# A streaming encoder layer on one core: last super-block's key and value rows through VectorE and DRAM, its last two projections unsplit, its last row tile scaled on two engines

## The chip, the cores and the metric

The kernel runs on one core of a Trainium2 chip. The core has a matrix engine (TensorE, "PE" in the profile, with its weight loads as "PEld"), VectorE (DVE), ScalarE (ACT), GpSimd (POOL), a queue engine SyncE (SP) that issues almost all transfers here, and 16 DMA engines. The metric is the device time of one execution in microseconds; less is better. Every engine works through its own queue of instructions in order and waits on semaphores of the others.

## The reference

One layer of a hybrid encoder over 2048 prompt frames and 64 frames of a running stream. A combined projection feeds two groups of heads; their gated outputs are concatenated and projected back. The keys and values of the last 512 prompt frames are outputs too (`new_k_prompt`, `new_v_prompt`), in row order.

```python
aq, ak, av, ag, hq, hf, hi, hg = split(rms_norm(x, ln_g) @ w_in)   # x: 2048 (64) x 1024, w_in: 1024 x 4096
o_a = band_attention(aq, ak, av) * silu(ag)      # 8 heads x 64, chunks of 64 frames see 8 chunks back
o_b = rms_norm(gla_recurrence(silu(hq), 1 - f, hi, log f)) * silu(hg)   # 4 heads x 128, f from sigmoid(hf)
y   = rms_norm(x + concat(o_a, o_b) @ w_out)     # also returned: the last 512 rows of k and v, the states
```

## The kernel before

**Stages.** The frames are cut into four super-blocks of 512 frames (the second has the 64 sample frames as well, `SUPER`). In each, 32 projection jobs run, listed in `JOBS`: for each of four recurrence heads the jobs hf, hq, hi, hg, and for each of four pairs of attention heads pg (gate), pq, pk, pv. A job is 24 accumulating matmuls with 128 features as the stationary operand and up to 512 frames as the moving one (`project`, L539): activations and weights are each split in a high and a low part, and three of the four products are summed. The result lands transposed, features on partitions and frames along the row, in one of two accumulator banks ("acc"), and an `ev_...` function takes it out. Matmuls of attention and recurrence are woven between the projection's. In the last super-block the jobs of the last pairs come in another order: hf3, hq3, pv2, pq2, pk2, hi3, hg3, pg2, pv3, pq3, pk3, pg3. Then the output projection runs for all eight tiles of 256 rows (`steps`, with seven products of a Strassen-like scheme for each), its sums are added to the residual rows on VectorE and GpSimd, and `out_norm` squares, normalizes and stores each tile of 128 rows.

**What sets the order.** All instructions are emitted by one Python program (`Plan`) that keeps a model clock with costs for each engine, and threads (generators) that ask for tokens. `tk["sig"]` and the like count the buffers of a tag; a thread takes a token before it uses a buffer, and `put(1, t)` gives it back at model time `t`. So the planner's due times fix the order of each engine's queue; on the chip, semaphores wait for the real event. Tags that matter here: "sig" (two buffers of 128x512, used by the exponentials of the gates and of hf, hq and hg, and as staging for output rows), "vT" (three such buffers, used by q, k, v and the recurrence's inputs), "ck" (one buffer, used for the squares of the norms among others), "tr" (two PSUM banks for transposes), "kv0" and "kv1" (the one set of key and value tiles, given on from pair to pair).

**Keys and values in the first three super-blocks.** `ev_k` (L790) copies the accumulator to a vT tile and splits it for both heads into the key tile. `ev_v` needs frames on partitions, so it transposes 32x32 blocks on VectorE (`turn_blocks`, L666), sends them through a DRAM scratch called "way" with four writes and one read back (`turn_rows`, L677, L691 and L695), and splits the rows (`split_rows`, L657). The recurrence's inputs (hi) take the same way.

**In the last super-block**, `ev_v_last` (L811) copies the values to a vT tile and turns them on TensorE, four half-height transposes for each head, and `new_rows` (L624) turns the whole tile once more, four transposes of 128x128, copies the result to a sig tile (L645) and stores it with one transfer (L650). `ev_k` calls the same `new_rows` for the keys. The sig token comes back as soon as the store is issued.

**The last two jobs** of every super-block (and its first two) run in two halves of 256 frames: job n-2 first half, job n-1 first half, then both second halves, so that the next super-block's activations can replace the first half early.

**The end.** For the last pair of row tiles, `out_norm` scales each tile's two 512-wide halves one after the other on VectorE, by the row's factor and by the gain, and SP stores each half (L1898, L1901).

Of the kernel before, what the change touches and what calls it, by code (L numbers as in the profile page):

```python
# [183 lines left out]
def hymba_step(  # L184
# [439 lines left out]
    def new_rows(src, off, bn, p, out_p, out_s, tok, t):  # L624
# [15 lines left out]
        for a, b, rows, out in segs:  # L640
            s3 = pt[:rows, a * P : b * P].rearrange("p (t d) -> p t d", d=P)
            yield from tk["sig"].get()
            yield "D", t
            st = T(wk, [P, 512], F32, "sig", bufs=2).rearrange("p (t d) -> p t d", d=P)
            dve.tensor_copy(st[:rows, : b - a], s3)  # L645
            t = C.dve((b - a) * P)
            yield t
            row = off + a * P
            if rows == P:
                sp.dma_start(out[row : row + (b - a) * P, p * P : (p + 1) * P].rearrange("(t q) d -> q t d", q=P),  # L650
                             st[:, : b - a])
            else:
                sp.dma_start(out[:, p * P : (p + 1) * P], st[:rows, 0])
            tk["sig"].put()
        tk["tr"].put(1, t)

# [82 lines left out]
    def pair_jobs(sb, p):  # L739
        t0, n = SUPER[sb][:2]  # L740
        last = sb == len(SUPER) - 1
        smp = n > WIN
# [47 lines left out]
        def ev_k(acc, off, bn, t):  # L790
# [17 lines left out]
            yield from new_rows(kn, off, bn, p, nk_prompt if last else None, nk_sample, tk["vT"], t)  # L808
# [31 lines left out]
        def ev_v(acc, off, bn, t):  # L840
# [9 lines left out]
            for c, w, rows, out in parts:  # L850
                if out is not None:
                    rows_out(vt[:rows, c : c + w], out, slice(p * P, (p + 1) * P), t)
            for h in range(2):
                yield lambda: d.open[h]
                for c, w, rows, _ in parts:
                    yield "A", t
                    t = yield from split_rows(vt[:rows, c : c + w], d.v, h, 4 + (off + c) // P, w // P, rows, t)
                d.v_n[h] += bn
                d.v_t[h] = max(d.v_t[h], t + 500.0)
            tk["vT"].put(1, t)  # L860
# [43 lines left out]
        return d, dict(g=ev_g, q=ev_q, k=ev_k, v=ev_v_last if last else ev_v)  # L904
# [956 lines left out]
    def out_norm(o, tile_, half, t):  # L1861
# [11 lines left out]
        if tile_ not in o["first"]:  # L1873
# [5 lines left out]
            o["b0"][tile_] = b0  # L1879
            return  # L1880
# [6 lines left out]
        if x[3] is not None and not end:  # L1887
# [5 lines left out]
            C.dma(512 * rows / P)  # L1893
        else:
# [56 lines left out]
    def program():  # L1951
# [66 lines left out]
        for sb in range(nsb):  # L2018
# [6 lines left out]
            for u, (kind, g) in enumerate(JOBS[sb]):  # L2025
# [16 lines left out]
                if u in (1, len(JOBS[sb]) - 1):  # L2042
# [7 lines left out]
                elif u not in (0, len(JOBS[sb]) - 2):  # L2050
                    yield from project(j, blocks, evac)
                before = evac
# [149 lines left out]
```

## Time and profile before

| what | value |
|---|---|
| median of 3 runs | 1247.86 us (1247.58 to 1248.82) |
| the profiled execution's own time | 1248.42 us |
| its span, first to last instruction | 1246.1 us |
| mean granted TensorE clock | 0.999 |
| TensorE busy | 99% of the span, 7494 matmuls |
| VectorE, ScalarE, GpSimd busy | 72%, 55%, 33% |
| DMA, queue of SP | 289.86 MB, 69.0% of 16 engines' time |

The profile lists for each group of instructions the line of the kernel that issued it, the engine, the operation, the output and input tiles, and the shape; then the busy time, the mean duration of one, and the idle time ahead of it with what ended that. The time line has start, duration, engine, line and count of merged instructions. Matmuls overlap in the pipeline, so what one costs in a stream is the distance between starts and not its duration.

### The profile page before, as it was taken

To read this page: it belongs to the slowest core of one execution; us is meant where nothing else is said; L and a number is where in the kernel's file an instruction comes from. 1 tells how busy PE (TensorE), PEld (TensorE's weight loads), DVE (VectorE), ACT (ScalarE), POOL (GpSimd) and SP (SyncE) were. 2 spreads that over 40 slices of the span, in tenths; PEclk is the share of its full clock that TensorE was granted. 3 is DMA by queue.
4 is the path that set the end of the run, shared out by engine and by line. 5 is a ranking of instruction groups with operands and counts; after the bars stand their busy time and mean duration, and the time that the engine had idled before them with its cause. 6 is when DMAs were issued, how large, how long until landed. Compare 5 with 4: busy or idle time off the path is not lost. (4 is left out here: it accounts for less than half of the span.)

```text
span 1246.1 us, 21403 instructions
## 1 busy us (share of the span) xinstructions
PE 1234.7 (99%) x7494; PEld 1085.9 (87%) x7494; DVE 893.0 (72%) x1901; ACT 683.0 (55%) x1534; POOL 413.2 (33%) x702
## 2 busy tenths in 40 slices
PE   9999999999999999999999999999999999999997
PEld 7888888999999999998888888988888888888786
DVE  7697878867767677786577667776757476867775
ACT  6354545755665556574465556665556445643443
POOL 7665564111120111201233242143242103474543
PEclk9999999999999999999999999999999999999999
DMA  8897888667575575655777778677686665988431
GB/s 337 301 321 258 320 293 327 204 185 252 155 217 148 158 252 186 204 164 189 279 267 251 271 263 281 227 257 252 231 273 206 218 209 208 343 266 245 144 118 68
DMA packets 144516, 291.22 MB, mean 234 GB/s; under 512 B 38617, under 2 KB 85337, under 8 KB 126746
## 3 DMA queue, kind: packets, MB, share of 16 engines
q1 hardware_dynamic: 144120, 289.86, 69.0%
q8 instruction: 59, 0.97, 0.3%
q14 instruction: 47, 0.39, 0.1%
q10 hardware_dynamic: 290, 0.01, 0.0%
HBM read 196.95 MB, written 93.91 MB: 233 GB/s over the span
## 5 line engine op out<-in xcount | busy, mean ns | idle before, releaser
L249 PE MATMUL acc<-xh,w 128*128 128x512 f32 (+2 forms) x2752 | 566.0, 345 | 1.2 <-DVE gq L580 0.7
L249 PEld LDWEIGHTS acc<-xh,w 128*128 128x128 f32 x2752 | 438.4, 189 | 51.7 <-ACT xh L409 0.9
L249 PE MATMUL acc<-xl,w 128*128 128x512 f32 (+2 forms) x1376 | 293.8, 345 | 0.5 <-DVE xl L415 0.5
L249 PEld LDWEIGHTS acc<-xl,w 128*128 128x128 f32 x1376 | 221.0, 189 | 25.2 <-DVE xl L415 0.7
L939 ACT ACTIVATE pr<-pr,nm 128x640 f32<-128x640 f32 (+4 forms) x132 | 100.4, 761 | 56.3 <-DVE nm L922 55.9
L951 ACT CAST ph<-tr 128x512 fp32r<-128x512 f32 (+3 forms) x176 | 87.8, 506 | 74.8 <-PE pv L249 50.1
L922 DVE CUSTOM_DVE_ANT_0 pr<-s,bias 128x640 f32<-128x640 f32 (+4 forms) x128 | 94.3, 737 | 46.6 <-PE s L249 45.7
L473 POOL TENSOR_TENSOR w<-wraw,w 128x256 fp32r<-128x256 f32 x120 | 102.3, 882 | 54.9 <-DVE w L468 41.8
L954 DVE TENSOR_TENSOR ph<-tr,ph 128x512 fp32r<-128x512 f32 (+3 forms) x176 | 100.8, 588 | 25.0 <-ACT ph L951 24.3
L249 PE MATMUL pv<-ph,v 128*128 128x256 f32 (+2 forms) x344 | 97.1, 368 | 0.0
L510 POOL TENSOR_TENSOR xn<-wraw,xn 128x256 fp32r<-128x256 f32 x48 | 41.2, 859 | 145.0 <-ACT xn L507 145.0
L253 PE MATMUL tr<-ident,pr 128*128 128x128 f32 x580 | 88.3, 273 | 0.3 <-DVE ph L954 0.3
L1570 POOL TENSOR_TENSOR k<-ob 128x512 f32<-128x512 f32 (+2 forms) x20 | 18.0, 902 | 198.4 <-ACT ob L1561 157.3
L1095 POOL TENSOR_TENSOR mixa<-mixa,sga 128x256 f32<-128x256 f32 (+1 forms) x36 | 28.0, 779 | 167.1 <-DVE mixa L993 141.4
L993 DVE TENSOR_TENSOR mixa<-mixa,pv 64x256 f32<-64x256 f32 (+1 forms) x144 | 56.8, 394 | 35.7 <-ACT mixa L989 32.2
L943 DVE TENSOR_SCALAR pr<-pr,sm 128x640 f32<-128x640 f32 (+4 forms) x132 | 75.8, 574 | 4.7
L253 PEld LDWEIGHTS tr<-ident,pr 128*128 128x128 f32 x580 | 69.6, 140 | 9.9 <-PE acc L249 0.7
L575 ACT ACTIVATE sig<-acc 128x512 f32<-128x512 f32 (+2 forms) x64 | 32.0, 500 | 76.4 <-PE acc L249 73.7
L249 PEld LDWEIGHTS pv<-ph,v 128*128 128x128 f32 (+1 forms) x344 | 58.6, 189 | 7.4 <-issue 0.3
L989 ACT COPY mixa<-pv 64x256 f32<-64x256 f32 (+1 forms) x72 | 25.1, 349 | 64.3 <-PE pv L249 58.4
L249 PE MATMUL s<-kd,q 128*128 128x320 f32 (+2 forms) x232 | 55.6, 309 | 0.0
L249 PE MATMUL s<-kd,ql 128*128 128x320 f32 (+2 forms) x232 | 55.5, 309 | 0.0
(338 smaller groups left out, 2131.2 us busy)
## 6 DMA issues: line engine op xcount, KB each, us to landing
w<-wd SPq DMA_DIRECT2D x96, 1024.0 KB, 5.4
wd<-w SPq DMA_DIRECT2D x32, 1024.0 KB, 7.1
wraw<-in_w_in_dram SPq DMA_DIRECT2D x30, 512.0 KB, 5.0
wod<-xn SPq DMA_DIRECT2D x28, 512.0 KB, 5.0
xn<-in_x_prompt_dram SPq DMA_DIRECT2D x23, 512.0 KB, 4.7
bias<-biasd SPq DMA_DIRECT2D x24, 320.0 KB, 5.8
carry<-kd SPq DMA_DIRECT2D x12, 512.0 KB, 5.8
carry<-v SPq DMA_DIRECT2D x12, 512.0 KB, 6.2
```

The costliest lines, as they stand in the source:

```text
L249: pe.matmul(out, w, x, **kw)
L253: pe.transpose(out, x, idn)
L473: pool.tensor_sub(w[:, 1, k : k + 2], raw[:, k : k + 2], f32(w[:, 0, k : k + 2]))
L510: pool.tensor_sub(f32r(st[:, c.start + 512 : c.stop + 512]), src[:, c], st[:, c])
L575: act.activation(sig[:, :bn], acc, AF.Exp, scale=-1.0)
L922: dve.tensor_tensor_reduce(s[:, :nk].rearrange("p (a c) -> p a c", a=ns), sps[:, :ns, :kn], d.bias[:, h, bcol : bcol + nk].rearrange("p (a ...
L939: act.activation(s[:, :nk], s[:, :nk], AF.Exp, bias=nm[:, 0:1], scale=-1.0, accum_out=sm)
L943: dve.tensor_scalar(s[:, :nk], s[:, :nk], sm, None, ALU.mult)
L951: act.copy(ph[:krows, 0, :wid], pt[:krows, :wid])
L954: dve.tensor_sub(ph[:krows, 1, :wid], pt[:krows, :wid], f32(ph[:krows, 0, :wid]))
L993: dve.tensor_add(mix[hs, :qn], mix[hs, :qn], pv[hs, i, :qn])
L1095: pool.tensor_mul(mix[:, :n], mix[:, :n], d.sg[:, g0 : g0 + n])
```

## The change

Four edits, all in the last super-block and behind it.

1. For its pairs 0, 1 and 2 (`by_blocks`) the values take `ev_v`, the way through DRAM, in place of `ev_v_last`, and the rows for the output are stored straight from the turned vT tile by the new `rows_to`: four transfers of 128 rows x 128 columns, in pieces of 32 columns. The keys' rows take the new `block_rows`: block transpose into a sig tile, the way through DRAM, then `rows_to`. Pair 3 keeps the transposes on TensorE.
2. In `new_rows`, the value rows of pair 3 are staged in "ck" and no longer in "sig", and the staging token comes back 6 model microseconds after the store.
3. The last two jobs of the last super-block run whole, 512 frames at a time.
4. For the last row tile, the half that is finished first is multiplied by the gain ahead of time; when the row factor is there, ScalarE scales that half and issues its store, and VectorE scales the other half, stored by SP.

```diff
@@ new_rows
-            yield from tk["sig"].get()
+            tag = "ck" if out is nv_prompt else "sig"
+            yield from tk[tag].get()
...
-            st = T(wk, [P, 512], F32, "sig", bufs=2).rearrange("p (t d) -> p t d", d=P)
+            st = T(wk, [P, 512], F32, tag, bufs=1 if tag == "ck" else 2).rearrange("p (t d) -> p t d", d=P)
...
-            tk["sig"].put()
+            tk[tag].put(1, C.now + (6000.0 if rows == P else 0.0))
...
+    def rows_to(src, out, off, w, p):
+        s4 = src.rearrange("q (a t j) -> q t a j", a=4, j=32)
+        for i in range(w // P):
+            row = off + i * P
+            sp.dma_start(out[row : row + P, p * P : (p + 1) * P].rearrange("q (a j) -> q a j", a=4), s4[:, i])
+            C.dma(64)
+            yield C.now + 800.0
+
+    def block_rows(src, off, bn, p, out, tok, t):
+        yield from tk["sig"].get()
+        yield "D", t
+        st = T(wk, [P, 512], F32, "sig", bufs=2)
+        t = turn_blocks(st, src, bn)
+        tok.put(1, t)
+        t = yield from turn_rows(st, bn, t)
+        yield t
+        yield from rows_to(st[:, :bn], out, off, bn, p)
+        tk["sig"].put(1, C.now + 4000.0)
@@ pair_jobs
+        by_blocks = last and p < NPAIR - 1
@@ ev_k
+            if by_blocks:
+                yield from block_rows(kn, off, bn, p, nk_prompt, tk["vT"], t)
+            else:
+                yield from new_rows(kn, off, bn, p, nk_prompt if last else None, nk_sample, tk["vT"], t)
@@ ev_v
+                elif by_blocks:
+                    C.spawn(rows_to(vt[:, c : c + w], nv_prompt, off + c, w, p), 2)
...
-            tk["vT"].put(1, t)
+            tk["vT"].put(1, t + (4000.0 if by_blocks else 0.0))
@@ pair_jobs, its result
-        return d, dict(g=ev_g, q=ev_q, k=ev_k, v=ev_v_last if last else ev_v)
+        return d, dict(g=ev_g, q=ev_q, k=ev_k, v=ev_v_last if last and not by_blocks else ev_v)
@@ out_norm
+            if end and tile_:
+                yield "D", 0.0
+                c = slice(half * 512, half * 512 + 512)
+                dve.tensor_mul(x[half], x[half], g_in[:, c])
+                C.dve(530)
+                o["scaled"] = half
...
+        elif end and tile_:
+            a = o["scaled"]
+            act.mul(x[a], x[a], r)
+            act.dma_start(y[:, a * 512 : a * 512 + 512], x[a])
+            c = slice((1 - a) * 512, (1 - a) * 512 + 512)
+            dve.scalar_tensor_tensor(x[1 - a], x[1 - a], r, g_in[:, c], ALU.mult, ALU.mult)
+            sp.dma_start(y[:, c], x[1 - a])
@@ program
-                if u in (1, len(JOBS[sb]) - 1):
+                if u == 1 or (u == len(JOBS[sb]) - 1 and not last):
...
-                elif u not in (0, len(JOBS[sb]) - 2):
+                elif u != 0 and (last or u != len(JOBS[sb]) - 2):
                     yield from project(j, blocks, evac)
+                    if u == len(JOBS[sb]) - 1:
+                        x_left[sb, 0] = x_left[sb, 1] = True
```

More of the change, by code (lines that the diff above doesn't have):

```diff
@@ L807, in ev_k @@
                 d.k_t[h] = max(d.k_t[h], t)
-            yield from new_rows(kn, off, bn, p, nk_prompt if last else None, nk_sample, tk["vT"], t)
+            if by_blocks:
+                yield from block_rows(kn, off, bn, p, nk_prompt, tk["vT"], t)
+            else:
+                yield from new_rows(kn, off, bn, p, nk_prompt if last else None, nk_sample, tk["vT"], t)
             yield from got_all(True)
```

## The prediction

> **What bounds the kernel now.** I read the page's first part, then the busy times by window, then TensorE's waits, and only then single instructions in the time line.
>
> ```profile
> span 1246.1 us, 21403 instructions
> ...
> PE 1234.7 (99%) x7494; PEld 1085.9 (87%) x7494; DVE 893.0 (72%) x1901; ACT 683.0 (55%) x1534; POOL 413.2 (33%) x702
> ```
>
> ```profile
> core 0: us, PE busy (x) PEld busy (x) DVE busy (x) ACT busy (x) POOL busy (x), PEclk, DMA share, GB/s
> 860.00:1064.00 204.00, 204.00 (x1186) 174.46 (x1185) 135.02 (x277) 111.11 (x227) 51.94 (x89) 1.00 0.67 227
> 1064.00:1142.00 78.00, 77.44 (x371) 63.84 (x370) 57.15 (x104) 41.16 (x97) 46.92 (x58) 1.00 0.89 292
> 1142.00:1240.00 98.00, 96.35 (x421) 77.46 (x419) 67.95 (x105) 39.39 (x99) 47.69 (x54) 1.00 0.36 118
> 640.00:848.00 208.00, 208.00 (x1278) 181.81 (x1278) 150.21 (x307) 127.73 (x276) 62.88 (x103) 1.00 0.75 256
> ```
>
> ```profile
> engine line waited for: us in total, times, longest us
> PE acc L249 <- DVE pr L1821: 0.8, 1, 0.8
> ```
>
> From 860 to 1064 us, where the last super-block's projections and most of its attention run, TensorE is busy 204.00 of 204.00 us at clock 1.00, while VectorE is busy for 135 and ScalarE for 111. In the two output windows behind it, it misses 0.56 and 1.65 us, and its longest single wait is 0.8 us. A busy TensorE could hide waits, so I check by spacing, below: eight 512-wide matmuls take 1.82 us, 0.227 us each, with no room in them. So TensorE's instruction stream sets the end up to 1240, and a microsecond taken out of it is a microsecond, unless something new comes late. After that there is a tail of 6 us on other engines.
>
> **Transposes that leave TensorE.** Per pair the old code turns the keys' rows in 4 transposes of 128x128, the values in 8 of 64x128 and their output rows in 4 of 128x128. Three of the four pairs lose all 16. The price is not the duration but the spacing of starts.
>
> ```profile
> L253 PE MATMUL tr<-ident,vT x68: 221/271/300, 303.1 to 1066.1; 128*128 128x128 f32 x32, 64*128 64x64 f32 x32, 128*64 128x128 f32 x4
> ```
>
> ```profile
> 927.22 0.63 PE L249 MATMUL g<-q,ones 128*128 128x512 f32 x2
> 927.68 0.60 PE L253 MATMUL tr<-ident,vT 128*128 128x128 f32 x4
> 928.04 0.71 PE L249 MATMUL acc<-xh,w 128*128 128x512 f32 x2
> 928.58 0.46 PE L249 MATMUL s<-kd,q 128*128 128x320 f32 x2
> ...
> 931.55 0.46 PE L253 MATMUL tr<-ident,vT 64*128 64x64 f32 x4
> 931.94 0.56 PE L249 MATMUL s<-kd,q 128*128 128x320 f32 x2
> 932.34 0.46 PE L249 MATMUL s<-kd,ql 128*128 128x320 f32 x2
> 932.63 0.61 PE L249 MATMUL acc<-xh,w 128*128 128x512 f32 x2
> ```
>
> Four transposes start at 927.68 and the next matmul at 928.04: 0.36 us. But the two matmuls behind them take 0.54 instead of the 0.46 that two such take ahead of them, so the group costs 0.44. The half-height group takes 0.39 and lengthens the next two from 0.29 to 0.40: 0.50. A pair has two groups of each: 2 x 0.44 + 2 x 0.50 = 1.88 us, three pairs 5.64 us (bare spacing alone: 4.50, the low bound). The 68 of the first row are 16 per pair for four pairs, and 4 of sample keys that stay.
>
> The Trainium skill (TensorE: Matmul & The Clock Gate, Part 4: PE-mode transpose) has about 275 ns for a 128x128 transpose in one kernel's context. The trace agrees with that as a duration (median 271 ns), but in a stream the durations overlap; by the page's figure 48 of them would be an estimated 13.2 us and the profiled time 1233.9 us.
>
> **Last two jobs whole.** The last two jobs each run in two 256-wide halves: 96 matmuls instead of 48 of 512.
>
> ```profile
> 899.66 1.98 PE L249 MATMUL acc<-xl,w 128*128 128x512 f32 x8
> 901.48 1.98 PE L249 MATMUL acc<-xh,w 128*128 128x512 f32 x8
> ...
> 1059.18 2.08 PE L249 MATMUL acc<-xh,w 128*128 128x256 f32 x16
> 1061.10 1.12 PE L249 MATMUL acc<-xl,w 128*128 128x256 f32 x8
> ```
>
> A narrow one takes 1.92/16 = 0.120 us, a wide one 1.82/8 = 0.2275: 11.52 against 10.92, a gain of 0.60 us. Whole keys reach the first scores of pair 3 later and the last ones earlier; the queued output products are there as cover, so nothing for that (it would cost at most the 1.92 us of the 16 narrow matmuls that now stand before them).
>
> **The tail.** The last row tile's two halves are scaled one after the other on VectorE.
>
> ```profile
> 1237.47 0.15 DVE L1877 TENSOR_SCALAR b<-ss 128x1 f32<-128x1 f32 x1
> ...
> 1239.66 0.69 DVE L1821 TENSOR_TENSOR pr<-pr,acc 128x512 f32<-128x512 f32 x1 [2.05 <-issue]
> ...
> 1241.70 1.42 DVE L1898 SCALAR_TENSOR_TENSOR pr<-pr,rstd,gin 128x512 f32<-128x512 f32 x2
> 1242.52 0.96 SPq L1901 DMA_DIRECT2D out_dram<-pr  x2
> ```
>
> ```profile
> out_dram<-pr SPq DMA_DIRECT2D x2, 256.0 KB, 2.1
> ```
>
> ```profile
> 0.83 0.52 ACTq L1959 DMA_DIRECT2D gin<-in_ln_in_g_dram  x1
> ```
>
> ```profile
> L1725 ACT CAST xh<-wraw 128x512 fp32r<-128x512 f32 x6 | 3.7, 622 | 4.8 <-PE acc L249 4.4 <-DMA wraw<-mixd 0.4
> ```
>
> With the change one half stays on VectorE, about 0.72 of the 1.42 us, and the other is a 128x512 pass on ScalarE, nearest row 0.62 us, started by the same event. Both stores then go out about when the first does now, so the second's 0.7 us goes: I take 0.67. The low bound is 0: ScalarE's own issue took 0.52 us at the start, and no row has a large store from its queue. The added multiplication by the gain (about 0.7 us) falls behind the row at 1237.47, into the 2.05 us in which VectorE idles ahead of 1239.66; without that cover it would cost 0.7.
>
> **What the detour adds.** A key or value tile now goes VectorE block transpose, four writes, one read, then four row writes, each of 64 KB in 128-byte pieces. The old way had one store, so SP's queue gets 8 more issues per tile, 48 in all. The nearest rows are the same detour of the recurrence's inputs in this super-block, and the scratch tile's other users:
>
> ```profile
> 989.35 0.57 ACT L815 COPY vT<-acc 128x512 f32<-128x512 f32 x1
> ...
> 1007.27 0.72 DVE L671 STREAM_TRANSPOSE vT<-acc 128x512 f32<-128x512 f32 x1 [0.51 <-PE acc L249]
> 1008.01 1.80 SPq L691 DMA_DIRECT2D way<-vT  x4
> 1008.61 0.69 DVE L645 COPY sig<-tr 128x512 f32<-128x512 f32 x1 [0.63 <-PE tr L253]
> 1013.96 0.34 SPq L695 DMA_DIRECT2D vT<-way  x1
> 1019.35 0.63 ACT L1279 COPY gi<-vT 128x512 f32<-128x512 f32 x1
> 1027.38 0.60 ACT L575 ACTIVATE sig<-acc 128x512 f32<-128x512 f32 x1
> ```
>
> ```profile
> 1065.56 0.38 ACT L575 ACTIVATE sig<-acc 128x256 f32<-128x256 f32 x1 [1.95 <-DMA out_dram<-sig]
> ```
>
> ```profile
> out_dram<-sig SPq DMA_DIRECT2D x7, 256.0 KB, 5.8
> ...
> out_dram<-vT SPq DMA_DIRECT2D x4, 32.0 KB, 1.8
> ```
>
> ```profile
> SPq L446 <- PE acc L249: 250.8, 69, 12.0
> ```
>
> Work on the engines is even: a 0.72 us transpose stands for a 0.69 copy. Values are usable 12.1 us after the turn (1007.27 to 1019.35) and no longer right behind TensorE's transposes; what can stand in front of them is projection work, as in 640 to 848, where all four pairs take this way and TensorE is busy 208.00 of 208.00. I take 0 for the delay; its other end is in the rivals. SP has 48 more issues at 0.45 (1.80/4), 22 us, against 250.8 us that its weight loads alone spend waiting for TensorE: 0. The transfers: DMA share is 0.67 in this window; a 32 KB write in 128-byte pieces lands in 1.8 us, so 24 of twice that size add at most 24 x 3.6 = 86 us to 204 x 0.67 = 137, just over the window; the 1.8 is mostly not occupancy, so I take no cost, with rival 2 as its other end. The last pair's value rows in another tile remove part of the 1.95 us wait on ScalarE, which cannot have held TensorE longer than the 0.56 us that it misses in the window from 1064 to 1142: a gain of 0 to 0.56, taken as 0.
>
> **Sum.** 5.64 + 0.60 + 0.67 = 6.9 us. The profiled execution took 1248.42 us (span 1246.1 and 2.3 around it): 1241.5. The median of the runs shown is 1247.86, lower by 0.56: **1241.0**.
>
> **Rivals.** A measurement of this kernel can tell about 0.2%, 2.5 us: below 1245.4 is faster, above 1250.4 slower.
>
> 1. Part is eaten. The key tile sits in one of two scratch buffers through detour and stores. Chain: 12.1 us, four stores 0.8 apart as the planner spaces them (3.2), landing 1.8 to 5.8: 17.1 to 21.1. If the buffers alternate, the next user but one needs it: from pair 2's key rows at 1008.61 to its gate at 1027.38 are 18.8 us. ScalarE would wait up to 2.3 us per pair. The value tile, one of three buffers, is as tight: 17.9 us from pair 2's copy at 989.35 to the turn at 1007.27, and there VectorE would wait. The 1.95 us wait above cost TensorE next to nothing, which speaks against. If half of 6.9 goes: 1244.4. Chance 0.18.
> 2. Slower: the chain's read or row stores sit on SP behind a weight load that waits for TensorE, longest 12.0 us. The chain grows to some 29 to 33, ScalarE stands 10 to 14 us in front of the gate's exponent, and behind it the softmax and the copies out of two accumulators; about 2 us are absorbed. One pair so hit costs 10: 1241.0 + 10 = 1251; two, 1261. It decides from a chain of 23 us in all three pairs (2.3 lost in each), or 28 in one. Against: the planner puts the read where it expects the landing, and in 640 to 848 no such thing shows. Small pieces push this way. The Trainium skill (DMA: Bandwidth & Descriptors, Specifications) wants at least 512 B per piece for full rate; no row here separates that from the fixed time of a transfer. Chance 0.13.
> 3. The output stage is paced by its transfers (DMA share 0.89 from 1064 to 1142) and does not move up: only 0.60 and 0.67 remain, 1246.6. Against: its loads are released by TensorE's progress, so they move too. Chance 0.07.
> 4. Durations count and not spacing: 48 x 0.271 = 13.0, and with 1.27 more 1233.6. The 208.00 of 208.00 with four durations of 0.27 inside 0.36 us speaks against. Chance 0.03.
>
> Forecast 0.59 (on its own 1239 to 1243.5). **Range** 1237.5 to 1247.5: the low end allows a few microseconds of waits that vanish along with the transposes; the high end takes in rivals 1 and 3 and leaves out 2 and 4. **Chances**: faster 0.59 + 0.03 + 0.11 of rival 1 + 0.02 of rival 3 = 0.75; same 0.07 + 0.05 = 0.12; slower 0.13.
>
> **What would show it.** Right: transposes of vT fall from 68 to 20; TensorE's busy time falls by 5 to 7 us and its idle time stays near 11.4; no wait of TensorE over 1 us; the last stores are two, from SP and ScalarE, within 0.2 us of each other. Wrong: waits of ScalarE or VectorE on row stores to the outputs, over 3 us; TensorE waiting for the values, the probabilities or an accumulator between 860 and 1060; DMA share near 1 there.

## The result, and the profile after

The changed kernel takes 1247.22 us (median of 20 runs, 1244.23 to 1248.76), the kernel before on the same chips 1249.03 (20 runs, 1247.58 to 1250.28): ratio 0.9985, 95% interval 0.9978 to 0.9991. That is 1.9 us (1.1 to 2.7) less, where 6.9 was forecast. The time lies inside the range, at its upper end, which had been drawn to take in rivals 1 and 3. The profiled execution took 1245.85 us. I read it as I read the one before: the page's first part, the transposes, the windows, the waits, and then the end.

```profile
span 1244.1 us, 21258 instructions
...
PE 1229.7 (99%) x7398; PEld 1078.0 (87%) x7398; DVE 897.0 (72%) x1897; ACT 680.6 (55%) x1526; POOL 415.2 (33%) x702
```

```profile
L253 PE MATMUL tr<-ident,vT x20: 222/271/327, 302.3 to 1055.8; 64*128 64x64 f32 x8, 128*128 128x128 f32 x8, 128*64 128x128 f32 x4
```

The work has gone: 96 matmuls fewer, 20 transposes of vT tiles where there were 68, and TensorE is busy 5.0 us less. But the span is only 2.0 shorter, so TensorE's idle time has grown from 11.4 to 14.4. The busy times by window, in the cuts of the prediction, say where:

```profile
core 0: us, PE busy (x) PEld busy (x) DVE busy (x) ACT busy (x) POOL busy (x), PEclk, DMA share, GB/s
860.00:1064.00 204.00, 203.51 (x1122) 172.12 (x1121) 141.12 (x280) 109.71 (x223) 55.02 (x90) 1.00 0.77 252
1064.00:1142.00 78.00, 75.59 (x350) 60.57 (x349) 57.30 (x103) 39.34 (x94) 46.92 (x57) 1.00 0.83 276
```

TensorE stays full while the detour runs (203.51 of 204), but in the output stage behind it misses 2.41 us where it missed 0.56. Cut finer, it is two stretches, here 1060 to 1080 and 1100 to 1120, each with a DMA share near 1. The kernel before had shares of 0.90 and 0.91 there and a full TensorE, so the share alone does not tell why:

```profile
core 0: us, PE busy (x) PEld busy (x) DVE busy (x) ACT busy (x) POOL busy (x), PEclk, DMA share, GB/s
...
1060.00:1080.00 20.00, 18.98 (x100) 14.82 (x99) 16.63 (x37) 12.45 (x29) 10.66 (x13) 1.00 0.95 347
1080.00:1100.00 20.00, 20.00 (x100) 16.67 (x99) 13.76 (x29) 9.63 (x21) 16.02 (x21) 1.00 0.65 237
1100.00:1120.00 20.00, 18.61 (x80) 14.52 (x79) 14.48 (x19) 10.02 (x27) 9.50 (x11) 1.00 1.01 320
```

Before:

```profile
1060.00:1080.00 20.00, 20.00 (x118) 17.31 (x117) 14.86 (x37) 12.94 (x29) 6.11 (x8) 1.00 0.90 319
...
1100.00:1120.00 20.00, 20.00 (x89) 16.47 (x88) 13.42 (x19) 9.85 (x28) 15.33 (x19) 1.00 0.91 279
```

The single waits of TensorE there are short, 0.9 us at most: for VectorE's additions, for the probabilities, and 0.5 us for a weight to land. The prediction's signs of being wrong looked at 860 to 1060, where nothing of the kind shows; the loss lies behind.

**Two measures for the rest of the text.** A pipelined TensorE hides short waits in its busy time, so I take starts. For each shape of matmul I take the median distance to the next start in the kernel before. The sum over all matmuls is the *work*: 1207.96 us before, 1202.03 after, 5.93 less. What a distance has over its median is *stall*: 0.39 us before and 2.67 after in 1060 to 1080, 0.06 and 2.24 in 1100 to 1120. And since the profiles differ at 800 us already, ahead of any changed instruction (798.0 to 800.9 over all kernels here), a *lead* is counted from there. So counted the last matmul starts 2.44 us earlier than before: 5.93 less work, 3.5 more stall.

The end has grown too. The time line of the last instructions, after:

```profile
1234.12 0.75 DVE L1909 TENSOR_TENSOR pr<-pr,gin 128x512 f32<-128x512 f32 x1
...
1236.25 0.69 DVE L1847 TENSOR_TENSOR pr<-pr,acc 128x512 f32<-128x512 f32 x1 [1.38 <-issue]
...
1238.29 0.75 DVE L1931 SCALAR_TENSOR_TENSOR pr<-pr,rstd,gin 128x512 f32<-128x512 f32 x1 [0.69 <-ACT rstd L1916]
1238.96 0.75 DVE L1937 SCALAR_TENSOR_TENSOR bias<-bias,rstd,gin 128x512 f32<-128x512 f32 x1
1239.04 0.37 ACTq L1929 DMA_DIRECT2D out_dram<-pr  x1
1239.10 0.33 SPq L1932 DMA_DIRECT2D out_dram<-pr  x1
1239.53 1.27 SPq L1940 DMA_DIRECT2D out_dram<-bias  x2
```

From the last addition (1236.25) to the end of the span are 7.85 us; before they were 6.44 (1239.66 to 1246.1). Both of the last tile's stores leave within 0.06 us of each other, as the prediction wanted. But they are not the last: the other tile's second half is scaled behind them on VectorE (1238.96), and its stores stand behind them on SP, though its first half was ready at 1237.60. All four stores, 1 MB, now share the DMA engines after 1239.04. Before, two had left at 1241.04, 1.5 us ahead of the last two.

### The profile page after: what moved, and what is told of

Same layout as the page of the kernel before. It is cut to its first block, busy times and chain, and to the rows that moved or that the text cites. A ratio compares the mean times of both kernels' runs of the same rounds, so it can differ in the third digit from the quotient of the medians.

```text
span 1244.1 us, 21258 instructions
## 1 busy us (share of the span) xinstructions
PE 1229.7 (99%) x7398; PEld 1078.0 (87%) x7398; DVE 897.0 (72%) x1897; ACT 680.6 (55%) x1526; POOL 415.2 (33%) x702
## 2 busy tenths in 40 slices
DMA packets 158324, 294.36 MB, mean 237 GB/s; under 512 B 51657, under 2 KB 98377, under 8 KB 140554
## 3 DMA queue, kind: packets, MB, share of 16 engines
q1 hardware_dynamic: 157784, 292.74, 70.3%
## 4 chain that ended last, share of the span: by engine, by line
PE 87%; DMA 4%; DVE 4%; issue 2%; ACT 2%; POOL 1%; SPq 0%; DVEq 0%; POOLq 0%; ACTq 0%
PE acc L249 62%; PE g L249 7%; PE pv L249 6%; PE tr L253 5%; PE s L249 5%; DMA w<-wd 1%; DMA out_dram<-ck 1%; DMA way<-vT 1%; POOL sig L1777 1%; DMA vT<-way 1%; DMA mixd<-ob 1%; PE g L253 1%; DMA mixd<-mixa 0%; DMA bias<-wind 0%; DVE xn L1847 0%
```

## The experiments

| kernel | median, us | before, us | ratio | interval | lead of last matmul | stall 1060-1080 | stall 1100-1120 |
|---|---|---|---|---|---|---|---|
| after (edits 1-4) | 1247.22 | 1249.03 | 0.9985 | 0.9978-0.9991 | 2.4 | 2.67 | 2.24 |
| e1: edit 1 | 1247.76 | 1249.17 | 0.9988 | 0.9979-0.9997 | 0.5 | 2.05 | 0.04 |
| e2: edit 3 | 1268.63 | 1249.17 | 1.0153 | 1.0139-1.0167 | -19.1 | 6.02 | 9.93 |
| e3: edit 4 | 1250.11 | 1249.17 | 1.0005 | 0.9996-1.0014 | -1.6 | 0.76 | 0.41 |
| e4: edit 2 | 1250.40 | 1249.17 | 1.0009 | 1.0000-1.0018 | -2.0 | 0.49 | 0.08 |
| e5: 1-4, tail's order | 1247.67 | 1249.27 | 0.9991 | 0.9982-1.0000 | 2.4 | 3.94 | 1.51 |
| e6: 1-4, own scratch | 1246.97 | 1249.27 | 0.9980 | 0.9971-0.9988 | 2.5 | 3.28 | 2.20 |
| e7: edits 2, 3 | 1268.03 | 1249.27 | 1.0151 | 1.0137-1.0164 | -19.7 | 5.42 | 10.51 |
| e8: edits 1-3 | 1246.12 | 1249.27 | 0.9974 | 0.9964-0.9984 | 3.3 | 2.46 | 2.19 |
| e9: 1-3, light | 1244.92 | 1248.64 | 0.9964 | 0.9952-0.9976 | 4.9 | 0.85 | 2.23 |
| e10: before, light | 1248.53 | 1248.64 | 0.9997 | 0.9989-1.0006 | 0.2 | 0.18 | 0.08 |
| e11: 1-3, gain later | 1244.69 | 1248.64 | 0.9970 | 0.9958-0.9982 | 3.8 | 2.56 | 1.64 |
| e12: edits 1, 3 | 1254.00 | 1248.64 | 1.0046 | 1.0033-1.0059 | -5.1 | 1.67 | 2.43 |
| e13: 1-3, split early | 1248.44 | 1249.48 | 0.9990 | 0.9982-0.9999 | 0.8 | 2.99 | 4.32 |
| e14: as e13, light | 1244.96 | 1249.48 | 0.9959 | 0.9947-0.9971 | 2.6 | 2.74 | 1.93 |
| e15: 1-3, softmax first | 1248.93 | 1249.48 | 0.9991 | 0.9983-1.0000 | 1.1 | 6.25 | 0.46 |
| e16: e13 and e15 | 1248.52 | 1249.48 | 0.9993 | 0.9984-1.0001 | -1.8 | 6.92 | 0.04 |
| e17: 1-3, rows left out | 1245.62 | 1248.81 | 0.9971 | 0.9960-0.9981 | 2.3 | 2.00 | 2.24 |
| e18: 1-3, gain early | 1245.43 | 1248.81 | 0.9968 | 0.9955-0.9980 | 2.7 | 2.91 | 2.22 |

The ratio and its interval are worked out from all runs and need not be the quotient of the two medians. The last three columns (us; a negative lead is a delay) are of one profile each and the medians are not: compare e14, whose profile has 2.6 us of lead and whose median is 4.5 us below that of the kernel before. A profile says which wait there is; how much it costs only the medians say.

The stall has a second source in seven of the profiles: the clock that TensorE is granted falls from 1.00 to 0.50 for a while. It does so in e1 for 6.8 us from 1057.5, in e12 for 6.8 us from 1064.0, in e13, e15 and e16 for 3.4 us from 1114.0, 1074.9 and 1078.0, and in e2 and e7 twice, for 3.4 us near 1073 and for 13.7 us near 1117. In each of these profiles a single wait of TensorE of 1.9 to 7.9 us ends within 1 us of such a fall or lies across it; in the others, from 20 us on, no wait is longer than 1.7 us. In e1 the mean clock shows the fall (the column behind POOL's):

```profile
1050.00:1060.00 10.00, 6.88 (x49) 6.23 (x48) 8.61 (x19) 5.89 (x14) 8.22 (x10) 0.88 0.81 297
1060.00:1070.00 10.00, 10.00 (x57) 9.48 (x57) 6.08 (x16) 5.08 (x12) 1.43 (x2) 0.78 0.41 116
```

Into the stretches at 0.50 fall 2.7 us of stall in e1, 1.6 in e12, 1.4 to 1.5 in e13, e15 and e16, and 11.9 and 12.6 in e2 and e7, with the waits that lie in them. In all other profiles, of the kernel before and the changed one too, the clock is 1.00 from 14 us to the last matmul. So the large losses below are waits and a slower clock together, and the 3.5 us of the changed kernel are not of this kind.

### The edits one by one

```diff
+        by_blocks = last and p < NPAIR - 1
...
-        return d, dict(g=ev_g, q=ev_q, k=ev_k, v=ev_v_last if last else ev_v)
+        return d, dict(g=ev_g, q=ev_q, k=ev_k, v=ev_v_last if last and not by_blocks else ev_v)
```

> The kernel before with edit 1 alone: pairs 0 to 2 take the detour, everything else is old. Theory A (TensorE's work leaves as priced, and what is lost is lost through the ck staging and the order of the last stores): 4 to 5.5 us faster than before. Theory B (the detour brings waits of its own, or the output stage cannot follow): 0 to 2 us faster. As forecast, 5.64 us faster.

1.5 us faster (0.9988), in theory B's range. TensorE's work falls by 5.30 us, and at the last projection jobs the lead is there. Then it is lost between 1040 and 1080: 6.5 us of stall against 0.8, some of it at the clock of 0.50. TensorE's waits there, by what came last:

```profile
PE acc L249 <- ACT vT L814: 1.9, 1, 1.9
...
PE tr L253 <- DVE v L855: 1.2, 1, 1.2
```

Both lines are pair 3's own evacuation, which keeps the old way and comes in halves of 256.

```diff
-                if u in (1, len(JOBS[sb]) - 1):
+                if u == 1 or (u == len(JOBS[sb]) - 1 and not last):
...
-                elif u not in (0, len(JOBS[sb]) - 2):
+                elif u != 0 and (last or u != len(JOBS[sb]) - 2):
```

> The kernel before with edit 3 alone: the last two projections unsplit. Forecast and theory A: 0.6 us faster. Theory B, in which the output stage is held by its loads and by the end of pair 3's attention: 0, or slower if the scores of pair 3 come later.

19 us slower. The work falls by 0.62 us as priced, but the planner now emits pair 3's attention behind more output products: its last matmul starts at 1119.26 in place of 1098.91. The last two weights, which go into attention's tiles, are issued at 1119.28 and 1120.13 (before: 1097.29 and 1099.59). So TensorE waits for the softmax and then for weights, with the clock at 0.50 from 1117.98 to 1131.63:

```profile
PE acc L249 <- DMA ph<-wod: 4.9, 1, 4.9
PE pv L249 <- DVE ph L954: 4.0, 2, 3.8
PE tr L253 <- DVE b L1877: 2.9, 1, 2.9
```

```diff
+            if end and tile_:
+                yield "D", 0.0
...
+        elif end and tile_:
+            a = o["scaled"]
```

> The kernel before with edit 4 alone: the last row tile scaled by two engines. Forecast: 0.67 us faster. Theory A (the planner puts the first store of the tile ahead behind those of the last tile on SP, and the four last stores are bound by their 1 MB): 1 to 1.5 us slower, and from the last matmul's start to the end 8.3 us and not 6.9.

No gain: 1.0005, not clear of noise. From the last matmul's start to the end are 8.3 us, as in the changed kernel and in theory A; before, 6.9.

```diff
+            tag = "ck" if out is nv_prompt else "sig"
+            yield from tk[tag].get()
```

> The kernel before with edit 2 alone: value rows of pair 3 staged in ck, staging tokens back 6 model microseconds later. Forecast: 0 to 0.56 us faster. Theory A (the first square of the output norm waits on ScalarE for the store out of ck, with the softmax queued behind it): 0 to 1.5 us slower, and a ScalarE wait on the ck store of 2 us or more in the profile.

1.2 us slower, at the edge of what can be told (1.0000 to 1.0018); the stall, 2.78 us, sits in 1080 to 1100. Theory A's time came and its reason did not: in this profile ScalarE waits nowhere for the store out of "ck".

The four single results add up to some 19 us slower. The change as a whole is 1.9 us faster. So the edits work on each other, and two pairs were tried.

### Pairs of edits, and the tail

```diff
-            yield from tk["sig"].get()
+            tag = "ck" if out is nv_prompt else "sig"
+            yield from tk[tag].get()
...
-                if u in (1, len(JOBS[sb]) - 1):
+                if u == 1 or (u == len(JOBS[sb]) - 1 and not last):
```

> Edits 2 and 3 together (last pair's value rows staged in the other tile, last jobs whole), without the detour and with the old tail. Theory (the 19 us of whole jobs alone come from the row tiles: with both last jobs whole, the last pair's rows and its attention's tile wait for one another's two row tiles, and the plan puts the attention behind output products): with the other tile freed for it, the attention ends before 1101 us as in the kernel before, time 1247.5 to 1251. Rival (whole jobs alone bring the last pair's q, k, v evacuations late whatever tile the rows use, and it is the detour that mends it): the attention still ends after 1110, time 1260 to 1270.

Still 18.9 us slower: attention ends at 1117.39. My theory of the row tiles falls; with the old tail and the detour added (e8, below) it ends at 1095.76. The detour mends it; through which of the planner's tokens, I did not separate.

```diff
+        by_blocks = last and p < NPAIR - 1
...
-                if u in (1, len(JOBS[sb]) - 1):
+                if u == 1 or (u == len(JOBS[sb]) - 1 and not last):
```

> Edits 1 and 3 alone: detour and whole last jobs; the last pair's value rows staged in a row tile as before, old tail. Theory (the two belong together: the detour alone loses its gain to the last jobs' halves, whole jobs alone put pair 3's attention 19 us late, and edit 2 does neither good nor harm): 1245.5 to 1246.8. Rival (edit 2 is what keeps whole jobs from the 19 us): above 1258.

5.4 us slower, at neither expected value. Without edit 2 the value rows of pair 3 need the row tile that the key rows' store has not left yet, and it is VectorE that waits, with pair 3's gate and softmax behind it. TensorE waits 7.9 us for VectorE's work on the gate, and its clock is at 0.50 from 1063.95 to 1070.78:

```profile
DVE sig L645 <- DMA out_dram<-sig: 8.9, 1, 8.9
```

```profile
1055.09 0.95 SPq L2089 DMA_DIRECT2D w<-wod  x2
1056.67 10.73 SPq L650 DMA_DIRECT2D out_dram<-sig  x2
```

The first of the two stores was issued right behind a weight of 2 MB, and the second could follow only when it had landed. So edit 2, costed at nothing, is worth some 8.5 us once edits 1 and 3 are in (5.4 us above the kernel before without it, 3.2 below with it, in e8); the wait and the slow clock behind it are both in this.

```diff
-            if end and tile_:
-                yield "D", 0.0
...
-        elif end and tile_:
-            a = o["scaled"]
```

> The changed kernel with edit 4 undone (the last row tile scaled and stored as before), edits 1 to 3 kept. Theory (edit 4 costs 1.4 us between the last matmul and the end): last matmul to end 6.9 us, time 1245.6 to 1246.2. Rival (the longer tail is chance of that profile, or was there without the edit): last matmul to end 8 or more, time 1247.0 to 1247.6.

1246.12: with edit 4 undone the gain is 3.2 us and no longer 1.9. From the last addition to the end are 6.55 us again (1235.85 to 1242.4). The theory holds: edit 4 costs 1.3 to 1.4 us by the medians and ratios, where it was to save 0.67. (The two intervals, of e8 and of the changed kernel, overlap a little.)

```diff
-                yield "D", t
+                if not end:
+                    yield "D", t
                 dve.scalar_tensor_tensor(x[a][:rows], x[a][:rows], r[:rows], g_in[:rows, c], ALU.mult, ALU.mult)
...
-                yield t
+                if not end:
+                    yield t
```

> The changed kernel, with the first tile of the last row's scaling emitted as one piece, so that both of its stores and its second multiply stand ahead of the last tile's on SP and DVE; nothing else. Theory (the split tail is planned out of order: the first tile's second multiply stands behind the last tile's on DVE, its stores behind the last tile's on SP, and four 256 KB stores then share the DMA engines after the last matmul): last matmul to end of span goes from 8.3 us back to 6.3 to 6.9, time 1245.2 to 1245.8 beside 1247.2 of the changed kernel. Rival (the end is set by how many bytes are left, not by their order): last matmul to end stays within 0.3 of 8.3, time 1246.9 to 1247.5.

The theory misses: the stores now leave in the wanted order, but the time does not fall (0.9991). From the last matmul to the end it is 8.34 us, the rival's number, though not for the rival's reason. Its last instructions:

```profile
1238.05 1.42 DVE L1938 SCALAR_TENSOR_TENSOR bias<-bias,rstd,gin 128x512 f32<-128x512 f32 x2 [1.41 <-ACT rstd L1916]
1238.83 1.03 SPq L1942 DMA_DIRECT2D out_dram<-bias  x2
1239.38 0.15 DVE L1903 TENSOR_SCALAR b<-ss 128x1 f32<-128x1 f32 x1
1239.44 0.69 DVE L1909 TENSOR_TENSOR pr<-pr,gin 128x512 f32<-128x512 f32 x1
1240.04 0.68 DVE L1847 TENSOR_TENSOR pr<-pr,acc 128x512 f32<-128x512 f32 x1
...
1242.82 0.37 ACTq L1929 DMA_DIRECT2D out_dram<-pr  x1
1242.89 0.33 SPq L1932 DMA_DIRECT2D out_dram<-pr  x1
```

Two scalings and the early multiplication now stand ahead of the last addition, which starts 1.8 us after the last matmul's start in place of 0.5. The more telling number is behind it. From the first of the last two stores to the end of the span (1246.6) are 3.8 us; before, with the second store 0.6 us later, they were 3.6 (1242.52 to 1246.1). The landings say the same: before, the two stores land 2.04 and 2.10 us after their issues, in e5 2.65 and 2.76, so from the first issue to the last landing it is 2.72 and 2.82. The second store's later issue was hidden under the first one's transfer, and there were no 0.67 us to win. With four stores together, the last lands 4.11 us after the first issue (1239.04 to 1243.15); how much of the added 1.4 us is the 0.5 MB more and how much the later issue of the last store, no run here separates. The rest up to the end of the span, 0.9 to 1.0 us, is the same in all three. The Trainium skill (DMA: Bandwidth & Descriptors, Anatomy of one DMA — SWDGE (gpsimd) path) gives about 2.0 us of fixed time for transfers issued by GpSimd, with the movement of the bytes on top. No run here shows that for SP and ScalarE: a whole 256 KB store of SP's lands within 2.04 us, its movement included.

### Where the lead goes in the output stage

```diff
-        yield from tk["ck"].get()
-        junk = T(wk, [P, D], mybir.dt.bfloat16, "ck", bufs=1)
+        junk = T(wk, [P, 512], mybir.dt.bfloat16, "junk", bufs=1)
```

> The changed kernel, with the throw-away output of the output stage's square sums in a tile of its own (128x512 bf16) in place of the tile that now also stages the last pair's value rows; nothing else. Theory (ACT waits 2.36 us at 1066.8 for that store to land and holds softmax copies behind it, and this delays pair 3's attention and with it the output stage): the ACT wait and the PE stalls of 1068 to 1073 go, the lead of the PE stream at output step 16 grows from 3.2 to 5 us or more, time 1245.0 to 1246.0. Rival (the PE stalls there are made good later, since the output stage waits for pair 3's attention and mixed rows in any case): stalls of 1068 to 1073 go but the lead at step 16 stays 3 to 3.6, time 1247.0 to 1247.5.

In the changed kernel ScalarE waits for the value rows' store to leave "ck" before it may square there:

```profile
1066.79 0.63 ACT L1896 ACTIVATE ck<-xn 128x512 bf16<-128x512 f32 x1 [2.36 <-DMA out_dram<-ck]
```

```profile
1058.05 8.67 DMA out_dram<-ck
```

Given a tile of its own, the square waits no more, and on ScalarE the wait for the next transfer takes its place:

```profile
1069.41 0.62 ACT L1751 CAST xh<-sig 128x512 fp32r<-128x512 f32 x1 [2.52 <-DMA sig<-mixd]
```

The stall is not smaller (3.28) and the time about that of the changed kernel. The theory falls. The rival's time fits, but the stall did not go, it moved: TensorE now waits 1.7 us for the probabilities.

```diff
-                sp.dma_start(f32(r), wod[k][:, part, c])
+                n = r.shape[1] if part == 0 or k == 0 else 1
+                sp.dma_start(f32(r)[:, :n], wod[k][:, part, c][:, :n])
...
-                mm(bank[1], m[a][:, kt], w(b, kt), 512, start=n == 0, stop=n == 11)
+                mm(bank[1], m[a][:, kt], w(b, 0 if b and k else kt), 512, start=n == 0, stop=n == 11)
```

> Edits 1 to 3 with the old tail (as in the run with the old tail), and of six of the seven low halves of the output stage's weights only a quarter is loaded (the products read that quarter four times; 4.7 MB fewer between 1035 and 1110 us; the output is not the reference's). The PE order and its products are unchanged. Theory (after the change the output stage comes earlier than its transfers can: PE stalls of 1060 to 1080 and 1100 to 1120 are weights and mixed rows landing late in a saturated DMA): the excess in those two stretches falls from 4.6 to under 1.5 us, and the time is 3 us or more below that of the old-tail run, 1242.0 to 1243.5. Rival (the stalls come from pair 3's softmax chain on ACT and DVE, and from DVE): excess stays above 3.5, time 1245.5 to 1246.3.

> The kernel before with the same quarter loads of low weight halves (output not the reference's): the control for the run before it. Theory: before the change the transfers came in time, so little moves: 1248.3 to 1249.3, last matmul within 1 us; the difference of the two light kernels is then 5.5 to 6.5 us, the work that was taken out. Rival: the difference stays 2.5 to 3.5 us, as with all weights loaded.

In e9's profile no engine but SP waits for a landing in the first stretch, its stall falls to 0.85, and the lead grows to 4.9. The kernel before gains nothing by the same (0.9997), as expected. That points to transfers as what takes back part of the gain, and only because the stage has moved up. But this profile is of the fastest of five runs (1242.00, median 1244.92). The second stretch does not care (2.23), the two light kernels differ by 3.6 us, which is nearly the rival's 2.5 to 3.5 and not the theory's 5.5 to 6.5, and e14, light too and profiled at its median, has 2.74 in the first stretch. By the runs, e9 gains 0.6 us more than e8 (medians) or 1.2 (ratios), with overlapping intervals. So transfers are a suspect here and not a shown cause.

One distance shows how both stretches count. From the last matmul of pair 3's attention to the 17th output product are 21.02 to 21.03 us in the changed kernel, e6, e8, e9, e17 and e18 (1096.28 to 1117.30 in the changed one), light or not, and 21.54 before; in e5 and e11, with 0.6 to 0.7 us less stall in the second stretch, 20.44. So the output stage moves up about as far as that attention ends earlier: 1.7 us in the changed kernel, 4.3 in e9. The projections, counted alike, end 7.4 us earlier. Of the 5.7 us between, 3.5 are no loss: ten matmuls of output products (108, before 98), four of scores and six transposes more stand between the last projection and attention's end. The other 2.2 are the stall of the first stretch.

```diff
-        rows_at[i] = (blocks, extra, tags, max(t, C.free["S"] + 2000.0))
+        t = max(t, C.free["S"] + 2000.0) + {1: 0.0, 2: -2500.0}.get(i, 0.0)
+        rows_at[i] = (blocks, extra, tags, t)
```

> Edits 1 to 3 with the old tail; the rows of the third output tile pair are planned 2.5 us earlier, so that on ACT and DVE their first split stands ahead of the second finished tile's norm. PE's order is the same. Theory (the stall of 1109 to 1117 is this order): excess in 1100 to 1120 falls from 2.2 to under 1.0 us, time about 1.2 us below the old-tail run, 1244.5 to 1245.3. Rival (those rows land only at about 1107 us, in a saturated DMA, so that ACT now waits for the landing with the norm behind it): excess stays 2 or more, time 1245.8 to 1246.8.

> The same order with the light weights (a quarter of six low halves loaded, output not the reference's): both stalls relieved. Theory: excess under 1.0 us in each of the two stretches; last matmul within 0.6 us of 5.9 us ahead of the kernel before, counted from the same point at 800 us, that is the work taken out; time about 1.2 us below the light run, 1242.5 to 1244. Rival (landing): as the light run, excess 2.2 in 1100 to 1120.

The rival is right as to the wait: put earlier, the splits of the third tile pair stand and wait for its rows, with the finished tile's norm behind them, and the stall is 4.32, of which 1.5 at the clock of 0.50. The time, 1248.44, is above the rival's too. With light weights (e14) the theory misses as well: stalls of 2.74 and 1.93, a lead of 2.6, and 1244.96.

```profile
1108.30 0.62 ACT L1752 CAST xh<-wraw 128x512 fp32r<-128x512 f32 x1 [1.93 <-DMA wraw<-mixd]
```

```profile
POOL wraw L1778 <- DMA wraw<-mixd: 4.9, 1, 4.9
```

In the changed kernel the same rows are issued at 1097.91, right behind the two last weights, 2 MB each, which go into attention's tiles and so can leave only when attention ends. By e13 they land some 8.8 us after their issue (1099.51 to 1108.30):

```profile
1094.01 0.32 SPq L1126 DMA_DIRECT2D mixd<-mixa  x1
1094.44 2.48 SPq L2103 DMA_DIRECT2D ph<-wod  x2
1096.97 0.90 SPq L2103 DMA_DIRECT2D v<-wod  x2
1097.91 3.02 SPq L1696 DMA_DIRECT2D wraw<-mixd  x2
```

Left in their place, the splits come behind the norm on VectorE, which is busy 9.28 of 10 us in 1110 to 1120 (before too), and TensorE waits for the additions that free its banks. Either way 2 us or more.

```diff
+        t = max(t, C.free["S"] + 2000.0) + {1: 3000.0, 2: 0.0}.get(i, 0.0)
...
+        junk = T(wk, [P, 512], mybir.dt.bfloat16, "junk", bufs=1)
```

> Edits 1 to 3 with the old tail; the rows of the second output tile pair are planned 3 us later, so that pair 3's softmax and transposed copies stand ahead of their splits on ACT, and the square sums write a tile of their own. Theory (the stall of 1060 to 1080 is ACT waiting for mixed rows and for the value rows' store in a saturated DMA with softmax behind it): excess there falls from 2.5 to under 1.2 us and the last matmul comes 0.8 us or more earlier. Rival (the weight that lands late holds PE in any case, and less is woven in): excess stays above 2, time 1245.8 to 1246.8.

> Both of these orders at full load, old tail: a version meant to beat both kernels. Theory: excess under 1.2 in each stretch, last matmul 5 us or more ahead of the kernel before from the same point at 800 us, time 1243 to 1244.5. Rival: one of the two stalls stays (2 us or more), time 1245 to 1246.5.

Both theories miss; the rivals' stalls are there, and the times lie above theirs too. In e15 ScalarE no longer waits for rows, but VectorE does, in pair 3's scores (below); in e16 ScalarE waits 4.7 us for the rows of the third tile pair. With fewer output products woven in, TensorE stands 3.7 us in front of the transposes of the probabilities in both. Here the softmax chain is what it waits for, and 6 to 7 us go in the first stretch, 1.4 and 1.5 of them at the clock of 0.50. Attention ends 3.9 us earlier in e15 and it is no use, since the products that were put off have to come after.

```profile
1069.06 0.82 DVE L948 CUSTOM_DVE_ANT_0 pr<-s,bias 128x640 f32<-128x640 f32 x1 [1.65 <-DMA sig<-mixd]
```

```diff
+            if rows == P and p == NPAIR - 1:
+                sp.dma_start(out[row : row + 1, p * P : (p + 1) * P], st[:1, 0])
+            elif rows == P:
```

> Edits 1 to 3 with the old tail; of the last pair's key and value rows only one row of each is stored (0.5 MB fewer at 1056 to 1058 us; these outputs are incomplete). The order of every engine is unchanged. Theory (the row tile's store must land before SP can issue the mixed rows' loads, and these land late in a saturated DMA): SP's wait ahead of those loads (7 to 8 us) shrinks to under 3, ACT has no wait over 0.5 us for a landing at 1064 to 1072, the excess of 1060 to 1080 falls from 2.5 to under 1.2 us, time 1244.3 to 1245.5. Rival (the 2 MB weight ahead of them sets both): excess 2 or more, time 1245.8 to 1246.8.

Between the two: no wait on "ck" is left, but SP still stands 5.2 us in front of the mixed rows until the one-row store has landed behind the 2 MB weight, and TensorE waits 1.0 us for that weight. Stall 2.00.

```diff
         yield lambda: (len(SUPER) - 1, 1) in x_left
-        sp.dma_start(g_in, ln_f_g.rearrange("(o d) -> o d", o=1).broadcast_to([P, D]))
...
             wo_load(k, flat4(hi[:, c], lo[:, c]))
+        sp.dma_start(g_in, ln_f_g.rearrange("(o d) -> o d", o=1).broadcast_to([P, D]))
```

> Edits 1 to 3 with the old tail, and the 0.5 MB broadcast of the last norm's gain issued behind the fourth and fifth weights, in place of ahead of the third weight. Theory (transfers pace the start of the output stage): the third weight lands about 1.3 us earlier, the stall at 1064 (0.8 to 1.3 us) goes, time 1245.0 to 1245.8. Rival (that stall is made good by the next): unchanged, 1245.9 to 1246.5.

```diff
+        sp.dma_start(g_in, ln_f_g.rearrange("(o d) -> o d", o=1).broadcast_to([P, D]))
         for k in (1, 2):
```

> Edits 1 to 3 with the old tail; the 0.5 MB broadcast of the last norm's gain is issued at about 1020 us, in place of 1055, where it stood ahead of the third weight. The order of PE and ACT is unchanged. Theory (bytes ahead of weight and mixed rows set the first stall): 1.3 us less of it, excess of 1060 to 1080 about 1.2 us, time 1244.5 to 1245.5, the best version. Rival: unchanged, 1245.8 to 1246.8.

With half a megabyte taken from in front of the third weight, early or late, the wait for that weight is gone in both, and the stall is not (2.56 and 2.91): TensorE waits a few microseconds later instead, for the probabilities and in front of their transposes. So e18 has the time of its theory and the stall of its rival, and e11's time is below both. The medians come out low all the same, 0.9970 and 0.9968 against e8's 0.9974, with overlapping intervals. These are the best versions found that load everything: 3.4 to 4.0 us faster than the kernel before. That is also below the changed one (0.9985), with intervals that just overlap.

## Why the prediction was wrong, step by step

**Transposes and whole jobs.** Right. 5.64 + 0.60 were forecast; the work fell by 5.93, of it 5.30 by the transposes (e1) and 0.62 by the whole jobs (e2). The work is itself counted by spacing, 5.30 over 48 or 0.110 us each, so the check is the time that passed: the last projection matmul starts 7.4 us earlier, and 7.3 us less of counted work stand ahead of it. At a duration of 0.271 each, 7.7 us more would have gone.

**"... a microsecond taken out of it is a microsecond, unless something new comes late."** This step failed, by its last clause. The spacing of the kernel before showed no room, and from that I took that the path belongs to TensorE alone and that the output stage would move up with it. But that stage had its transfers, its softmax chain and VectorE's additions only just in time, and was not examined for how early it could start. 3.5 of the 5.93 us came back as stall: 2.3 us more in 1060 to 1080 and 2.2 more in 1100 to 1120, and 1.0 less elsewhere. The queued output products, which the prediction named as cover for a later attention, did not cover it: some of them had to wait for their own weight (0.5 us in the changed kernel, 1.0 in e17, 1.7 in e16).

**The tail, 0.67 us.** Wrong in sign: the changed order cost 1.4 us between last addition and end, and e8 against the changed kernel gives about the same by medians and ratios. Two things in the estimate were wrong: the second store's 0.7 us lay under the first's transfer, and the scaling of the other tile, which I did not follow, got behind the last one. The multiplication by the gain did fall into VectorE's idle time, as forecast.

**The detour.** Right that it costs nothing visible. No engine waits for the row stores of pairs 0 to 2. What is waited for is the landing of the detour's read: by SP, up to 9.6 us, and by ScalarE, which splits the values, up to 5.5 us. TensorE kept its lead all the while (3.5 us of stall from 860 to 1040 in both kernels):

```profile
SPq L662 <- DMA vT<-way: 20.8, 3, 9.6
```

```profile
ACT v L680 <- DMA vT<-way: 7.4, 2, 5.5
```

So rivals 1 and 2, which put the loss there, fall. Rival 4 falls with the spacing.

**Rival 3**, an output stage that is paced by its transfers and does not move up, gave 1246.6. It came nearest, with a chance of 0.07. The argument against it, "its loads are released by TensorE's progress, so they move too", is where I went wrong: the last weights, and the rows queued behind them, leave only as pair 3's attention ends (1094.44 to 1097.91, above), and that end moved by 1.7 us. It is not the whole cause either, since moving bytes out of the way (e11, e17, e18) left the stall, and e9's gain over e8 is within overlapping intervals.

**Edit 2, taken as 0.** Alone it costs about 1 us, with edits 1 and 3 it saves some 8.5. And whole jobs, taken as 0.60, cost 19 us without the detour, waits and a slower clock together. That each edit can be priced in the trace of the kernel before and the prices added was an assumption that the prediction did not state.

**What adds up.** 6.9 forecast less 1.9 measured is 5.0. The tail is some 2 of it (0.67 not won, 1.3 to 1.4 lost), 0.3 is work that was priced too high, and the rest, 2.6, goes with the stalls (3.5 in the one profile). **Open** is what causes them, and what one would have to move to get them back: each wait that was taken away let another take its place, ScalarE's on "ck", ScalarE's or VectorE's on mixed rows, TensorE's on the third weight, the softmax chain itself.

## What to carry to other kernels

A busy engine's work is worth its time only as far as the next stage can start earlier: before adding up, look in that stage for what releases its loads, and take the smallest lead among them, not the lead of the stream. Where a program plans the order of all queues, price edits together: an edit worth nothing alone can be what keeps the others from losing 8.5 us. At the end of a kernel, count from the first of the last stores: here a second store that left while the first still moved cost nothing, and two more put behind them did.

## What the runs showed of the hardware

TensorE's granted clock fell to 0.50 for 3.41, 6.83 or 13.65 us at a time, in the seven profiles with a single wait of 1.9 us or more and in none of those with 1.7 or less. What sets the length, no run here shows.

A 256 KB store issued behind a 2 MB load took 8.67 us to land, where those at the kernel's end land in 2.1 (the prediction's row); the tile that it leaves is locked that long. Cut to one row of 512 bytes (e17), the store of the key rows just ahead of it still kept SP waiting 5.2 us for its landing, so the store's own size is not what makes it late. The four row stores of 64 KB in 128-byte pieces, which I feared, were issued in 2.04 us and landed in 1.9 to 3.6 us at the median:

```profile
out_dram<-vT SPq DMA_DIRECT2D x12, 64.0 KB, 1.9
out_dram<-sig SPq DMA_DIRECT2D x12, 64.0 KB, 3.6
```

The Trainium skill (DMA: Bandwidth & Descriptors, Specifications) wants 512 bytes per piece for full rate; packets under 512 bytes rose from 38617 to 51657 here, and the share of SP's queue from 69.0% to 70.3%, for 1.0% more bytes (289.86 to 292.74 MB). That agrees in direction, and no run here separates it from the detour's added bytes.
